# Output projection: three groups of elementwise instructions named for VectorE in place of GpSimd

## The chip, the cores and the metric

One core of a Trainium2 chip runs the whole program. The metric is device time in microseconds (us) of one launch, as the median of several runs. The core has five engines with a queue each: TensorE (in the profile PE, its weight loads PEld) for matrix products, VectorE (DVE) and GpSimd (POOL) for elementwise work, ScalarE (ACT) for copies, casts and activations, and SyncE (SP), which here only issues DMAs. An engine takes its instructions in the order in which they stand in its queue, and an instruction that waits holds everything behind it.

## The reference

The program computes one layer of a hybrid decoder for a prompt of 2048 tokens and for a group of 8 x 4 sampled tokens. Four groups of heads (a convolution, a pooling mixer, stick-breaking attention, cross-attention into memory) each give 512 columns; every group is multiplied by its gate, and what concerns this document is how the layer ends:

```python
mix = jnp.concatenate([y_c * jax.nn.silu(cg), y_p * jax.nn.silu(pg),
                       y_s * jax.nn.silu(sg), y_m * jax.nn.silu(mg)], axis=-1)
out = rms_norm(mix @ w_out, post_g)
return x + out, conv_new, pool_new, k, v
...
y_prompt = rms_norm(xp, final_g)
y_sample = rms_norm(xs, final_g)
```

So `mix`, 2048 (and 32) rows of 2048 columns, is multiplied by `w_out`, 2048 x 1024. The row is normalised and multiplied by the post factor `post_g`, the residual `x` is added, and a last normalisation with the factor `final_g` gives the output. Everything is float32.

## The kernel before

The program runs projections, the sampled group, the prompt's attention and then the output projection, one after another with overlaps; this document is about the last of these, from about 1905 us to the end.

**Seven products in place of eight.** The product `mix @ w_out` is split into 2 x 2 blocks (rows by pairs of 128-row tiles, the 2048 inner columns in halves, the 1024 output columns in halves) and done by the scheme of Strassen and Winograd: seven block products, numbered 1 to 7, of sums and differences of the blocks. Each runs over 8 pairs `i` of row tiles, plus `i = LAST = 8` for the 32 sampled rows, and over two halves `h` of its inner columns. One such `(prod, i, h)` is called a part. A part is 12 matrix products on TensorE (`out_part`, L2020): four blocks of 128 inner columns, each in three passes, since operands are split into a high and a low part (`mh` and `ml` for rows, `wohi` and `wolo` for weights) to keep float32 accuracy.

**What goes before a part.** `out_load` issues the DMA of its rows (`mr`) from DRAM on SP's queue: `mixd` holds `mix`, and `msd` holds differences that an earlier product has stored. `out_combine` makes the sum or difference that the product needs. `out_high` casts it on ACT (L1744, `mh`), `out_low` subtracts (L1755, `ml`, on DVE). In the main loop `prepare` does the load seven parts ahead of the part on TensorE, the combination five and the cast four; `lows` makes the low parts about three ahead. The combinations:

- product 6: L1735 on DVE subtracts in `ts[0]`, pinned behind what was traced on DVE before; L1736 on POOL takes this from a row kept since product 2, in `ts[2]`, which is stored to `msd` and becomes product 3's operand later. `store` issues that DMA on SP once more than two are pending.
- product 5: L1729 on POOL adds the two row halves that product 4's load has brought along (`ts[0] + ts[1]`), queued behind the last L1736 that was traced.
- product 7: L1732 on POOL, which stays as it is.

**What goes after it.** `out_ready` takes the accumulators from PSUM (L1788 to L1807, on DVE), and, where a half of an output tile is complete, has ACT sum its squares (`square`, L1759) and DVE multiply it by the post factor `gpost` (L1812). For the even tiles the left half was finished earlier, by product 2, and was put into DRAM (`c11d`). `out_first` loads it back into `oh` (two buffers), and `out_factor` multiplies it by the post factor: L1840, on POOL. `out_tile` then forms a tile: root of the sum of squares (L1856 to L1858 on DVE and ACT for tiles below 10, L1853 and L1854 on POOL for tiles 10 to 15, into `oss`), scaling and residual (L1864 on DVE), squares again (L1866, ACT), root, final factor (L1871, DVE), and the store.

**Order.** The program is traced part by part, and a planner then arranges each engine's queue by the order of tracing and by when it expects operands to be ready. `tc.keep_in_program_order(ins)` pins an instruction behind the one traced before it on the same engine; `tc.issue_after(ins)` queues what it encloses behind the given one. Anything else may be moved by the planner. The parts run in this order: products 1 and 7 over all `i`; 2 and 6 in turn; then, from `last_` on, 4, 5 and 3 in turn:

```python
order += [(4, 0), (4, 1), (5, 0), (5, 1), (4, 2), (5, 2), (3, 0), (3, 1), (3, 2), (5, 8), (3, 8)]
order += [(p, i) for i in range(3, 8) for p in (4, 5, 3)]
```

So in the last stage each pair of row tiles costs TensorE six parts: two of product 4, two of 5, two of 3.

Of the kernel before, what the change touches and what calls it, by code (L numbers as in the profile page):

```python
# [13 lines left out]
ALU = mybir.AluOpType  # L14
# [78 lines left out]
def kernel(  # L93
# [9 lines left out]
    pe, act, dve, pool, sp = nc.tensor, nc.scalar, nc.vector, nc.gpsimd, nc.sync  # L103
# [1540 lines left out]
    def store(key=None):  # L1644
        while len(stores) > 2 or key in [k for k, *_ in stores]:
            sp.dma_start(*stores.pop(0)[1:])
# [76 lines left out]
    def out_combine(x):  # L1723
        prod, i, h = x
        store()
        ts = raws[x]
        if prod == 5 and i < LAST:
            with tc.issue_after(keep["sixth"]):
                pool.tensor_tensor(out=ts[1], in0=ts[0], in1=ts[1], op=ALU.add)  # L1729
            ts = ts[1:]  # L1730
        elif prod == 7:
            pool.tensor_tensor(out=ts[0], in0=ts[0], in1=ts[1], op=ALU.subtract)  # L1732
            stores.append(((0, i, h), msd[0, i, h], ts[0]))
        elif prod == 6:
            tc.keep_in_program_order(dve.tensor_tensor(out=ts[0], in0=ts[0], in1=ts[1], op=ALU.subtract))  # L1735
            keep["sixth"] = pool.tensor_tensor(out=ts[2], in0=ts[2], in1=ts[0], op=ALU.subtract).ins  # L1736
            stores.append(((1, i, h), msd[1, i, h], ts[2]))
        raws[x] = ts[0]

# [21 lines left out]
    def out_ready(prod, i, o):  # L1761
# [35 lines left out]
        else:  # L1797
# [28 lines left out]
            if prod == 5 and i != 2 or (prod, i) == (3, 1):  # L1826
                out_factor(2 if prod == 3 else i)
# [9 lines left out]
        keep[2 * i, 0] = c  # L1837

    def out_factor(i):
        pool.tensor_tensor(out=keep[2 * i, 0], in0=keep[2 * i, 0], in1=gpost[:, :512], op=ALU.mult)  # L1840

    def out_tile(t, a, b):

# [130 lines left out]
    raws, mix, accs, keep, stores = {}, {}, {}, {}, []  # L1974
# [3 lines left out]
    def side_work():  # L1978
        nonlocal opm, conv
        with tc.tile_pool(name="sm", bufs=1, side="left", reuse_waits="tile") as sm2:  # L1980
            yield from sample_end(sm2, side_ps, S)
        with tc.tile_pool(name="wsp", bufs=1, side="left", reuse_waits="tile") as wsp:
            yield from weight_sums(wsp)
        opm = ox.enter_context(tc.tile_pool(name="opm", bufs=1, side="left", reuse_waits="tile"))
        yield from out_weights(1, opm, pool)
        while (3, 0) not in flags:
            yield
        for x in lead_:
            out_load(x)
            out_combine(x)  # L1990
            out_high(x)
            out_low(x, pool)
            yield

        while (3, 1) not in flags:
            yield
        for x in parts[2 * LEAD : 2 * LEAD + 3]:
            out_load(x)
        cp = cx.enter_context(tc.tile_pool(name="cp", bufs=1, side="left", reuse_waits="tile"))
        conv = conv_post(cp, lambda n: conv_ps[0](n), lambda: cx.enter_context(  # L2000
            tc.tile_pool(name="cpw", bufs=1, side="left", reuse_waits="tile")))
        while "centered" not in flags:
            next(conv)
            yield
# [55 lines left out]
    op = oy.enter_context(tc.tile_pool(name="op", bufs=1, side="right", reuse_waits="tile"))  # L2060
# [58 lines left out]
    def prepare(n):  # L2119
        for d, f in ((3, out_load), (1, out_combine), (0, out_high)):  # L2120
            for x in parts[: n + d]:
                if x in ready[d]:
                    continue
                prod, i, h = x
                if d == 3 and not h and prod == 2:
                    while i < LAST and ("conv", i) not in flags:
                        next(conv, None)
                    if i == LAST:
                        for _ in conv:
                            pass  # L2130
                f(x)
                ready[d].add(x)

    ready = {d: set(lead_ if d < 3 else parts[: 2 * LEAD + 3]) for d in (3, 1, 0, -1)}
    for n, x in enumerate(parts):
        if n == last_:
# [3 lines left out]
            gpost = ope.tile([P, D], F32, name="gpost", bufs=1)  # L2140
# [4 lines left out]
        prod, i, h = x  # L2145
# [55 lines left out]
```

## Time and profile before

| | |
|---|---|
| median of 3 runs | 2331.49 us (2330.65 to 2332.27) |
| the profiled execution: its time | 2334.9 us |
| its span | 2333.2 us |
| mean granted TensorE clock | 0.993 of full speed |
| first and last start of L1736 (POOL, x16) | 2053.1 and 2163.1 us |
| first and last start of L1729 (POOL, x16) | 2167.0 and 2275.8 us |
| first and last start of L1840 (POOL, x8) | 2180.3 and 2297.6 us |

Two kinds of views are used. A group line names the line of the kernel, the engine, the operation, output <- inputs and shapes; then `x` the count, `|` busy time in us, the mean of one in ns, `|` the idle time of the engine just before these, and what ended it. A timeline line is a start in us, a duration in us, the engine, the instruction, and in brackets the idle time before it with what ended it. Times are from the span's start. Busy times are those of instructions; an instruction that is held back by the hardware after its start shows as a longer one, and one that waits for another engine's signal shows as idle time in front of it.

### The profile page before, as it was taken

To read this page: it belongs to the slowest core of one execution; us is meant where nothing else is said; L and a number is where in the kernel's file an instruction comes from. 1 tells how busy PE (TensorE), PEld (TensorE's weight loads), DVE (VectorE), ACT (ScalarE), POOL (GpSimd) and SP (SyncE) were. 2 spreads that over 40 slices of the span, in tenths; PEclk is the share of its full clock that TensorE was granted. 3 is DMA by queue.
4 is the path that set the end of the run, shared out by engine and by line. 5 is a ranking of instruction groups with operands and counts; after the bars stand their busy time and mean duration, and the time that the engine had idled before them with its cause. 6 is when DMAs were issued, how large, how long until landed. Compare 5 with 4: busy or idle time off the path is not lost. (4 is left out here: it accounts for less than half of the span.)

```text
span 2333.2 us, 43434 instructions
## 1 busy us (share of the span) xinstructions
PE 2248.1 (96%) x16512; PEld 1810.3 (78%) x16512; DVE 1659.4 (71%) x2247; ACT 1125.2 (48%) x2031; POOL 1293.5 (55%) x1410
## 2 busy tenths in 40 slices
PE   7999999999999999999999999999999999999997
PEld 7998888898888777777777777666766668788775
DVE  5342786969747764478786868787877766686997
ACT  5332343242442322224242334699999976453553
POOL 3554545556474656545546455498988864332333
PEclk9999999999999999999999999999999999999999
DMA  6689987878778999987977884676554207876774
GB/s 205 206 283 310 339 272 258 287 249 287 246 257 310 307 357 334 334 279 271 318 255 236 296 274 145 171 217 175 153 137 130 73 24 250 274 223 204 237 243 145
DMA packets 338187, 558.31 MB, mean 239 GB/s; under 512 B 29162, under 2 KB 213610, under 8 KB 321580
## 3 DMA queue, kind: packets, MB, share of 16 engines
q1 hardware_dynamic: 282604, 286.83, 39.9%
q0 software_dynamic: 55376, 268.72, 32.6%
q8 instruction: 130, 2.13, 0.4%
q14 instruction: 77, 0.63, 0.1%
HBM read 465.35 MB, written 90.72 MB: 238 GB/s over the span
## 5 line engine op out<-in xcount | busy, mean ns | idle before, releaser
L990 DVE STREAM_TRANSPOSE T<-kt 128x1024 f32<-128x1024 f32 x256 | 308.7, 1226 | 188.1 <-PE sSA L1003 177.1
L957 POOL DMA_INDIRECT vt<-in_cache_v_dram,idv x256 | 252.0, 984 | 257.4 <-PE sO L1042 196.4
L642 DVE SCALAR_TENSOR_TENSOR cacc<-U,par,cacc 128x512 f32<-128x512 f32 x480 | 359.9, 750 | 11.0
L1375 POOL TENSOR_TENSOR be<-be,E 128x512 f32<-128x512 f32 (+4 forms) x316 | 300.9, 962 | 27.1 <-DVE E L1366 8.7
L1366 DVE TENSOR_TENSOR_SCAN E<-gam,cr,ZM 128x513 f32<-128x513 f32 x192 | 232.5, 1265 | 25.1 <-ACT gam L1296 22.0
L957 POOL DMA_INDIRECT kt<-in_cache_k_dram,idk x128 | 128.4, 1003 | 194.6 <-DVE T L990 150.1
L2020 PE MATMUL acc<-wohi,mh 128*128 128x512 f32 (+1 forms) x480 | 193.1, 402 | 0.2 <-ACT mh L1744 0.2
L2020 PE MATMUL acc<-wolo,mh 128*128 128x512 f32 (+1 forms) x480 | 189.0, 394 | 0.7 <-DVE wolo L1655 0.7
L2020 PE MATMUL acc<-wohi,ml 128*128 128x512 f32 x448 | 178.2, 398 | 8.9 <-DVE ml L1755 8.8
L1394 PE MATMUL AT<-ident,be 128*128 128x128 f32 x1082 | 150.7, 278 | 23.2 <-ACT at L1396 19.0
L1396 ACT COPY at<-AT 128x512 f32<-128x512 f32 (+1 forms) x288 | 162.3, 653 | 20.0 <-PE AT L1394 17.2
L1394 PEld LDWEIGHTS AT<-ident,be 128*128 128x128 f32 x1082 | 118.7, 141 | 66.2 <-issue 28.6
L1296 ACT ACTIVATE gam<-S 128x1024 f32<-128x1024 f32 (+1 forms) x158 | 163.4, 1034 | 7.3 <-PE S L1293 4.5
L1297 ACT ACTIVATE be<-S 128x1024 f32<-128x1024 f32 (+1 forms) x158 | 162.7, 1030 | 0.0
L1003 PE MATMUL sSA<-T,W 128*32 128x128 f32 x4096 | 139.6, 276 | 2.5 <-DVE T L990 1.4
L1406 PE MATMUL av<-at,V 128*64 128x256 f32 (+1 forms) x1152 | 135.7, 375 | 0.0
L1292 PE MATMUL S<-kh,Q 128*128 128x512 f32 (+1 forms) x316 | 132.1, 422 | 3.2 <-ACT be L1297 3.2
L1003 PEld LDWEIGHTS sSA<-T,W 128*32 128x32 f32 x4096 | 105.1, 109 | 38.4 <-issue 31.2
L1363 DVE TENSOR_TENSOR_SCAN E<-gam,ZM 128x384 f32<-128x384 f32 (+1 forms) x124 | 95.4, 814 | 53.7 <-ACT gam L1296 50.2
L1755 DVE TENSOR_TENSOR ml<-mr,mh 128x512 fp32r<-128x512 f32 x108 | 94.2, 879 | 42.9 <-ACT mh L1744 42.0
L1042 PE MATMUL sO<-vt,saT 128*32 128x512 f32 x1024 | 122.3, 592 | 0.0
L1406 PEld LDWEIGHTS av<-at,V 128*64 128x64 f32 x1152 | 75.8, 137 | 56.4 <-issue 24.2
(590 smaller groups left out, 6174.2 us busy)
## 6 DMA issues: line engine op xcount, KB each, us to landing
mr<-mixd SPq DMA_DIRECT2D x32, 512.0 KB
Q<-qd SPq DMA_DIRECT2D x96, 128.0 KB
mr<-mixd SPq DMA_DIRECT2D x48, 256.0 KB
xtp<-in_x_prompt_dram SPq DMA_DIRECT2D x16, 512.0 KB
kh<-kd SPq DMA_DIRECT2D x64, 128.0 KB
ws<-in_w_out_dram SPq DMA_DIRECT2D x16, 512.0 KB
wsd<-ws SPq DMA_DIRECT2D x16, 512.0 KB
msd<-mr SPq DMA_DIRECT2D x32, 256.0 KB
```

Source lines behind the costliest of these rows:

```text
L642: dve.scalar_tensor_tensor(out=ps, in0=U[:, a + k : a + k + H], scalar=wd[:, k : k + 1], in1=ps, op0=ALU.mult, op1=ALU.add)
L957: pool.indirect_dma_start(out=dst, out_offset=None, in_=rows, in_offset=bass.IndirectOffsetOnAxis(ap=idx, axis=0))
L990: S["turn"] = dve.transpose(T[:, 2 * hh : 2 * hh + 2].rearrange("p s j t -> p (s j t)"), kt[:, 2 * hh : 2 * hh + 2].rearrange("p s j d -> ...
L1003: pe.matmul(sSs[n][32 * g : 32 * g + 32, P * ml : P * (ml + 1)], lhsT=W[:, jj, :], rhs=T[:, :, jj, :], start=i == 0, stop=i == 3, tile_pos ...
L1296: act.activation(out=ga, in_=S[:, :, :w], func=AF.Sigmoid, scale=-1.0)
L1297: act.activation(out=be, in_=S[:, :, :w], func=AF.Sigmoid)
L1366: dve.tensor_tensor_scan(out=E[:, j][:, ::-1], data0=g_[:, j][:, ::-1], data1=ZM[:, 0:1].to_broadcast([P, 513]), initial=carry[hh, q2][:, ...
L1375: newest.append(pool.tensor_tensor(out=be[:, j, :m], in0=be[:, j, :m], in1=E[:, j, 513 - w : 513 - w + m], op=ALU.mult).ins)
L1394: pe.transpose(ap_[:, n : n + P], A[hp, qb, kc, hh, qt][:, P * r : P * (r + 1)], ident)
L1396: act.copy(at[:, :n], ap_[:, :n])
L1406: pe.matmul(av[64 * hh : 64 * hh + 64, c], lhsT=V[:, 4 * kc + r, 64 * hh : 64 * hh + 64], rhs=ats.pop((hp, qb, kc, hh, q2, r)), start=dg a ...
L2020: pe.matmul(o[:rows], lhsT=m[a][:, k, :rows], rhs=W[prod, 4 * h + k][w], start=not cont and h == k == n == 0, stop=h == 1 and k == 3 and n ...
```

## The change

The instruction of L1729 (16 of them), L1736 (16) and L1840 (8), all 128 x 512 float32 with both inputs in SBUF, is named for VectorE. The first two are pinned in the order of the program; the third isn't. With L1736 on DVE, the queueing of L1729 behind it falls away.

```diff
         if prod == 5 and i < LAST:
-            with tc.issue_after(keep["sixth"]):
-                pool.tensor_tensor(out=ts[1], in0=ts[0], in1=ts[1], op=ALU.add)
+            tc.keep_in_program_order(dve.tensor_tensor(out=ts[1], in0=ts[0], in1=ts[1], op=ALU.add))
             ts = ts[1:]
...
         elif prod == 6:
             tc.keep_in_program_order(dve.tensor_tensor(out=ts[0], in0=ts[0], in1=ts[1], op=ALU.subtract))
-            keep["sixth"] = pool.tensor_tensor(out=ts[2], in0=ts[2], in1=ts[0], op=ALU.subtract).ins
+            tc.keep_in_program_order(dve.tensor_tensor(out=ts[2], in0=ts[2], in1=ts[0], op=ALU.subtract))
             stores.append(((1, i, h), msd[1, i, h], ts[2]))
...
     def out_factor(i):
-        pool.tensor_tensor(out=keep[2 * i, 0], in0=keep[2 * i, 0], in1=gpost[:, :512], op=ALU.mult)
+        dve.tensor_tensor(out=keep[2 * i, 0], in0=keep[2 * i, 0], in1=gpost[:, :512], op=ALU.mult)
```

## What I expected before seeing the result

> **What bounds the kernel now.** I read the page first, then the table of stages for the last 283 us, then the waits of TensorE stage by stage, then the groups of instructions and the timelines of VectorE (DVE) and GpSimd (POOL).
>
> ```profile
> span 2333.2 us, 43434 instructions
> PE 2248.1 (96%) x16512; PEld 1810.3 (78%) x16512; DVE 1659.4 (71%) x2247; ACT 1125.2 (48%) x2031; POOL 1293.5 (55%) x1410
> ```
>
> The stages of the output projection, one line each:
>
> ```profile
> 2050.00:2160.00 110.00, 107.39 (x541) 89.52 (x540) 83.82 (x127) 48.50 (x99) 34.28 (x27) 0.98 0.71 219
> 2160.00:2218.00 58.00, 53.76 (x230) 42.14 (x229) 52.48 (x87) 31.41 (x72) 19.56 (x9) 1.00 0.73 235
> 2218.00:2250.00 32.00, 31.21 (x136) 23.41 (x134) 30.90 (x51) 16.63 (x45) 13.31 (x9) 1.00 0.77 259
> 2250.00:2284.00 34.00, 32.43 (x137) 25.52 (x138) 31.63 (x52) 16.57 (x45) 8.59 (x7) 1.00 0.64 217
> 2284.00:2320.00 36.00, 33.07 (x138) 25.07 (x136) 29.18 (x41) 15.54 (x40) 9.84 (x19) 1.00 0.43 153
> ```
>
> The columns are the stage and its length, then the busy time of PE, PEld, DVE, ACT and POOL, the granted clock, and DMA. TensorE is busy 96% of the span, so a change on other engines can only win what TensorE waits for. From 2160 to 2320 us it was idle 160 less 150.5, that is 9.5 us. DVE in the same four stages was busy 52.5 + 30.9 + 31.6 + 29.2 = 144.2 us of 160, thus 90%, while its share of the whole span is only 71%. These four stages are one: what DVE does is what TensorE waits for, as the waits of TensorE say, for the first, third and fourth of them:
>
> ```profile
> PE acc L2020 <- DVE ml L1755: 3.5, 3, 2.7
> PE acc L2020 <- DVE wolo L1655: 0.7, 1, 0.7
> ```
>
> ```profile
> PE acc L2020 <- DVE ml L1755: 2.4, 3, 1.5
> ```
>
> ```profile
> PE acc L2020 <- DVE ml L1755: 2.6, 4, 1.3
> ```
>
> The columns are the sum in us, the times and the longest. They add up to 9.2 us, nearly all of the 9.5; the second stage has no such row. In every case the low part of a product's rows (`ml`) or of a weight (`wolo`) came late from DVE. So 9.2 us, about 0.4% of the time, is on offer, and not more.
>
> **What POOL costs DVE today.** The timelines around one moved instruction, POOL's first, then DVE's:
>
> ```profile
> 2155.28 1.62 POOL L1736 TENSOR_TENSOR mr<-mr,mr 128x512 f32<-128x512 f32 x1 [2.69 <-DVE mr L1735]
> ```
>
> ```profile
> 2154.46 0.68 DVE L1735 TENSOR_TENSOR mr<-mr 128x512 f32<-128x512 f32 x1
> 2155.06 0.68 DVE L1655 TENSOR_TENSOR wolo<-wor,wohi 128x512 fp32r<-128x512 f32 x1
> 2155.66 1.78 DVE L1735 TENSOR_TENSOR mr<-mr 128x512 f32<-128x512 f32 x1
> 2157.38 0.68 DVE L1755 TENSOR_TENSOR ml<-mr,mh 128x512 fp32r<-128x512 f32 x1
> ```
>
> Undisturbed, DVE starts one 128x512 instruction every 0.60 us (2154.46, 2155.06, 2155.66), and each shows 0.68. The one that starts while POOL has its own two-input instruction shows 1.78: it is held 1.10 us. The same stretching shows in the groups of DVE for 2160 to 2320 us:
>
> ```profile
> L1755 DVE TENSOR_TENSOR ml<-mr,mh 128x512 fp32r<-128x512 f32 x50 | 42.5, 856 | 1.2 <-ACT mh L1744 0.8
> L1871 DVE SCALAR_TENSOR_TENSOR oxt<-oxt,oss,gfin 128x1024 f32<-128x1024 f32 x14 | 19.9, 1423 | 4.2 <-POOL oss L1854 4.2
> L1864 DVE SCALAR_TENSOR_TENSOR oxt<-acc,oss,oxt 128x512 f32<-128x512 f32 x21 | 15.0, 743 | 0.8 <-POOL oss L1854 0.7
> L1655 DVE TENSOR_TENSOR wolo<-wor,wohi 128x512 fp32r<-128x512 f32 x18 | 13.7, 776 | 2.1 <-ACT wohi L1650 2.1
> L1864 DVE SCALAR_TENSOR_TENSOR oxt<-oh,oss,oxt 128x512 f32<-128x512 f32 x7 | 8.3, 1193 | 0.7 <-POOL oss L1854 0.7
> L1856 DVE TENSOR_TENSOR oss<-ssk 128x1 f32<-128x1 f32 x10 | 2.3, 230 | 0.0
> L1856 DVE TENSOR_TENSOR oss<-oss 128x1 f32<-128x1 f32 x10 | 2.0, 196 | 2.2 <-ACT junk L1866 2.2
> L1780 DVE TENSOR_TENSOR both<-both,gpost 32x512 f32<-32x512 f32 x1 | 1.8, 1777 | 0.0
> L1871 DVE SCALAR_TENSOR_TENSOR oxt<-oxt,oss,gfin 32x1024 f32<-32x1024 f32 x1 | 1.3, 1262 | 0.0
> L1856 DVE TENSOR_TENSOR oss<-oss 32x1 f32<-32x1 f32 x1 | 0.1, 141 | 0.0
> ```
>
> Means above the undisturbed duration, times the count: `ml` 50 x (0.856 - 0.68) = 8.8; L1871 14 x (1.423 - 1.262) = 2.3; `wolo` 18 x (0.776 - 0.68) = 1.7; L1864 on `oh` 7 x (1.193 - 0.743) = 3.2; L1780 1.777 - 0.68 = 1.1; the two L1856 groups 0.9 + 0.55 = 1.4. That is **18.5 us** of DVE time lost. The two L1864 groups are the same operation: the one that reads an accumulator in PSUM keeps 743 ns, the one that reads SBUF twice averages 1193. In these 160 us POOL has three large groups, and all of them are what the change moves:
>
> ```profile
> L1729 POOL TENSOR_TENSOR mr<-mr 128x512 f32<-128x512 f32 x16 | 27.1, 1705 | 57.0 <-DVE mh L1755 33.3 <-DMA mr<-mixd 23.5
> L1840 POOL TENSOR_TENSOR oh<-oh,gpost 128x512 f32<-128x512 f32 x8 | 12.7, 1595 | 20.7 <-DMA oh<-c11d 11.1 <-DVE acc L1779 6.2 <-DVE ml L1755 3.4
> L1736 POOL TENSOR_TENSOR mr<-mr,mr 128x512 f32<-128x512 f32 x1 | 4.0, 3958 | 3.9 <-ACT junk L1759 3.9
> ```
>
> So 25 POOL instructions cost DVE 18.5 us, 0.74 each, though they aren't DVE's.
>
> **The change part by part.**
>
> *The subtraction for product 3 (L1736), 16 times, 15 of them in 2050 to 2160.* Groups of that stage, DVE and then POOL:
>
> ```profile
> L1755 DVE TENSOR_TENSOR ml<-mr,mh 128x512 fp32r<-128x512 f32 x27 | 25.2, 937 | 6.6 <-ACT mh L1744 6.2
> L1655 DVE TENSOR_TENSOR wolo<-wor,wohi 128x512 fp32r<-128x512 f32 x13 | 14.4, 1129 | 0.0
> L1735 DVE TENSOR_TENSOR mr<-mr 128x512 f32<-128x512 f32 x14 | 11.2, 808 | 0.0
> ```
>
> ```profile
> L1736 POOL TENSOR_TENSOR mr<-mr,mr 128x512 f32<-128x512 f32 x15 | 22.6, 1510 | 51.1 <-DVE mr L1735 47.6 <-issue 2.7 <-DMA c11d<-c 0.8
> ```
>
> Held time here: 27 x 0.257 + 13 x 0.449 + 14 x 0.128 = 14.6 us. POOL has other work in this stage as well; L1736 is 22.6 of its 34.28 busy us, so I give it two thirds, 9.6 us. Added: the new instruction reads what L1735 has just written, and a pair of that kind shows here:
>
> ```profile
> 2160.89 0.67 DVE L1769 TENSOR_TENSOR both<-both,acc 32x512 f32<-32x512 f32 x1
> 2161.59 0.68 DVE L1773 TENSOR_TENSOR both<-both,both 32x512 f32<-32x512 f32 x1
> ```
>
> 0.70 from start to start, so 15 x 0.70 = 10.5 us. The net is +0.9 us on a DVE that is idle 26 of 110 us there, in which TensorE lost only 2.6 us. I take nothing for it. If that cover failed, the cost would be the 0.9; if the held time alone counted, a gain up to the 2.6. Its store to DRAM leaves after a 0.7 us step in place of 1.5, which only helps the queue of SyncE (SP).
>
> *Sums (L1729, 16) and post factors (L1840, 8), with one last L1736: 25 in 2160 to 2320.* They read rows that came by DMA, not a neighbour's result, so the pitch is 0.60: 25 x 0.60 = 15.0 us added, 18.5 removed, **net -3.5 us**. But it is not spread evenly. POOL runs ahead of the products: in the last stage only one moved instruction was left on it, and it held an `ml` on DVE by 1.1 us:
>
> ```profile
> 2297.61 2.21 POOL L1840 TENSOR_TENSOR oh<-oh,gpost 128x512 f32<-128x512 f32 x1 [0.24 <-DMA oh<-c11d]
> ```
>
> ```profile
> 2298.60 1.76 DVE L1755 TENSOR_TENSOR ml<-mr,mh 128x512 fp32r<-128x512 f32 x1
> ```
>
> On DVE a sum is pinned behind the instruction traced before it, and both are traced five parts ahead of the product; as far as the order of the program holds, the sums of row blocks 6 and 7, four in all, and one to three factors come after 2284. That stage gets 5 to 7 instructions, 3.0 to 4.2 us, and is relieved of 1.1: +1.9 to +3.1, I take +2.5. The three stages before it get -3.5 - 2.5 = **-6.0 us**. TensorE waits for DVE there 3.5 + 0.7 + 2.4 = 6.6 us, so I count the 6.0 in full. In the last stage DVE has gaps that can hide some of the 2.5: L1871 alone waits 4.2 us for `oss`, a chain through ACT and POOL that a sum doesn't lengthen if it falls into the gap. I take half, +1.2. The last factor may fall into the 13 us after the last product, where it costs 0 to 0.6; I take 0, as its DMA has long landed.
>
> *Queues and waits.* No DMA is added and none is moved to another queue. The waits for the rows move from POOL to DVE: behind a sum on DVE stand the `ml` of the next parts, and TensorE waits for those. Bounds: nothing, where DVE comes to the sum after its DMA; up to the 23.5 + 11.1 us that POOL idled until a DMA, where DVE came as early as POOL did. I take nothing, since DVE is behind and not ahead, and keep a part of it as a rival. ACT makes the high part from the sum; a sum now lasts 0.7 in place of 1.7 us.
>
> *Sum:* -6.0 + 1.2 = -4.8 us. The profiled execution took 2334.9 us around its span of 2333.2; the median shown is 2331.49, and a difference of this kind carries over as it is: **2326.7 us**.
>
> **The rivals.**
>
> *All waits of TensorE go* (20%). If DVE's lag vanishes, the 9.2 us go, to **2322.3 us**. For it: 18.5 us is a low count, as rows of other shapes were left out; and the last stage inherits the lead won before. Against it: DVE has 15 us of new work in a stretch where it was idle only 15.8. [...]
>
> *The relief falls where nobody waits* (27%). A good part of the stretching lies in 2218 to 2250, which has no TensorE wait of its own, and the order of DVE's queue, planned anew, may put a sum in front of an urgent `ml`. If half of the 6.0 is won and the whole 2.5 is paid: -0.5; if the gaps help, -2.5. I set **2330.0 us**: within the 0.2%.
>
> *DVE stands at the head of its queue for a DMA* (13%, the other side). The factor isn't pinned, so the planner may let it float to where it expects its rows. The load on SP's queue, the factor on POOL and the tile on DVE that uses the result:
>
> ```profile
> 2278.08 0.32 SPq L1836 DMA_DIRECT2D oh<-c11d x1
> ```
>
> ```profile
> 2280.75 1.31 POOL L1840 TENSOR_TENSOR oh<-oh,gpost 128x512 f32<-128x512 f32 x1 [3.25 <-DMA oh<-c11d]
> ```
>
> ```profile
> 2294.03 0.75 DVE L1864 SCALAR_TENSOR_TENSOR oxt<-oh,oss,oxt 128x512 f32<-128x512 f32 x1 [0.34 <-POOL oss L1854]
> ```
>
> The rows land 2.7 us after issue, and POOL stood waiting for them 3.25 us; the tile that needs the result came 13 us later. If DVE takes the factors as early as POOL did, it inherits their 11.1 us of waiting, and with the relief of 3.5 the time is 2331.5 + 7.6 = **2339.1 us**. The point that decides: DVE must reach the instruction more than about 3 us before its rows land in several of the eight cases. Against it: the program traces the factor after the tile in front, over 5 us behind the load.
>
> That the instructions stay on POOL can't be: the engine is named in each edit.
>
> **How the numbers follow.** About 0.2%, 4.7 us, is what a measurement of this kernel can tell from no change; so faster begins at 2326.8 and slower at 2336.2. My forecast of 2326.7 has 40%; its own spread (2 to 7 us won) lies on both sides of that bound, and I count 25 of the 40 as faster. With the first rival's 20 that is 0.45 faster; the other 15 and the second rival's 27 are 0.42 within; the third's 13 slower. The range runs from 2321.0, just under all waits gone, to 2334.5: the second rival with 4.5 us more, as when one or two waits for rows strike. Outside it are the bulk of the third rival and a few per cent below.
>
> **What would show it.** The number of POOL instructions falls by 40, DVE's rises by 40. The groups L1755 and L1864 on `oh` in the last 160 us go to about 0.68 and 0.75 us, whatever the time does; if they stay stretched, the theory of held instructions is wrong. DVE's busy time in 2160 to 2320 falls by about 3.5 us. TensorE's waits for `ml` shrink before 2284 and not after it. Wrong would be: idle time of DVE in front of the sums or factors that ends with a DMA (third rival), or `ml` waits as before though the stretching is gone (second rival).

## The result and the profile after

| | before | after |
|---|---|---|
| median of the comparison, 6 runs each | 2331.32 us (2329.92 to 2336.15) | 2350.06 us (2347.12 to 2351.24) |
| the profiled execution | 2334.9 us | 2351.24 us |
| its span | 2333.2 us | 2349.5 us |
| ratio after to before | | 1.0066, 95% interval 1.0051 to 1.0081 |

The kernel became **slower**, by 15.4 us of 2331.3 by the ratio (11.9 to 18.9 by its interval; the two medians lie 18.7 us apart), where 4.8 us less was forecast. Of all executions in this document one was in a slow state, 3668.86 us at a granted clock of 0.557 (the kernel without the pin, below), and the ratios leave it out. The lines of the kernel after stand one lower than before from L1728 on: the sum is L1728, the factor L1839, the cast L1743, `ml` L1754, the post factor after a product L1811, the final factor L1870, the matrix products L2019.

The head of the page of after, and its table of stages (the columns as in the prediction):

```profile
span 2349.5 us, 43376 instructions
PE 2251.6 (96%) x16512; PEld 1815.8 (77%) x16512; DVE 1658.5 (71%) x2287; ACT 1127.5 (48%) x2031; POOL 1229.9 (52%) x1370
```

```profile
2160.00:2218.00 58.00, 57.52 (x251) 46.36 (x250) 54.60 (x103) 34.62 (x81) 0.00 (x0) 1.00 0.76 248
2218.00:2250.00 32.00, 23.78 (x93) 17.29 (x92) 25.06 (x50) 13.68 (x36) 0.00 (x0) 0.84 0.71 249
2250.00:2284.00 34.00, 29.51 (x121) 23.10 (x119) 26.58 (x51) 14.85 (x41) 0.00 (x0) 0.95 0.50 170
2284.00:2320.00 36.00, 31.84 (x130) 25.28 (x131) 25.89 (x39) 14.63 (x34) 5.99 (x14) 0.95 0.42 154
```

The change did what it says: 40 instructions fewer on GpSimd, 40 more on VectorE, and VectorE's total is 0.9 us lower in spite of them. Until 2218 us the kernel after is *ahead*: it was busy on TensorE for 57.52 of 58 us, against 53.76 before. Then it loses: from 2218 to 2250 it does 93 matrix products where the kernel before did 136. The granted clock falls too (0.84, 0.95, 0.95, against 1.00 in all four stages before). And VectorE, 90% busy in these stages before, is busy 26.58 of 34 us from 2250 to 2284: it has become idler. What TensorE waits for after 2160 us:

```profile
PE acc L2019 <- ACT mh L1743: 19.0, 5, 8.2
PE acc L2019 <- DVE ml L1754: 0.8, 2, 0.5
```

The waits for `ml`, 9.2 us with `wolo` before, are down to 0.8. In their place stand five waits for **`mh`**, ACT's cast, which no row of before after 2160 us shows. ACT runs 2031 instructions as it did, so something comes late to it.

**Where the five waits come from.** VectorE's timeline around the second of them. An eviction is the step that takes a product's accumulator from PSUM; the first line is that of (3,3), product 3 of row block 3, which completes tile 6, and the second that of (4,4):

```profile
2252.84 0.70 DVE L1806 TENSOR_TENSOR acc<-acc,U 128x512 f32<-128x512 f32 x1
...
2258.31 0.70 DVE L1806 TENSOR_TENSOR acc<-acc,U 128x512 f32<-128x512 f32 x1 [0.32 <-PE acc L2019]
...
2260.50 0.68 DVE L1839 TENSOR_TENSOR oh<-oh,gpost 128x512 f32<-128x512 f32 x1
2261.09 1.28 DVE L1870 SCALAR_TENSOR_TENSOR oxt<-oxt,oss,gfin 128x1024 f32<-128x1024 f32 x1
2262.29 0.68 DVE L1728 TENSOR_TENSOR mr<-mr 128x512 f32<-128x512 f32 x1
2263.71 2.50 DVE L1754 TENSOR_TENSOR ml<-mr,mh 128x512 fp32r<-128x512 f32 x4 [0.74 <-ACT mh L1743]
...
2268.51 0.69 DVE L1798 TENSOR_TENSOR U<-acc,U 128x512 f32<-128x512 f32 x1 [1.69 <-PE acc L2019]
```

The same moment on ACT, and on TensorE:

```profile
2263.06 2.18 ACT L1743 CAST mh<-mr 128x512 fp32r<-128x512 f32 x4 [3.09 <-DVE mr L1728]
```

```profile
2260.60 0.39 PE L2019 MATMUL acc<-wohi,ml 128*128 128x512 f32 x1
2263.73 0.50 PE L2019 MATMUL acc<-wohi,mh 128*128 128x512 f32 x1 [2.75 <-ACT mh L1743]
```

Read from the bottom up. TensorE has finished part (5,4,0) and wants (5,4,1). Its cast starts at 2263.06 and is the first of four that ACT had queued one behind the other (those of the two parts of product 3 and of (4,5,0) follow it): ACT stood idle 3.09 us for the sum. The sum of (5,4,1) started at 2262.29 straight behind an L1870 at 2261.09, by the program's order the final factor of tile 6; it is pinned there, since it is traced when the even tile of the row block in front has just been traced. And L1870 is the end of a tile that starts from a product of TensorE. So there is a loop: **when the eviction of (3,3) starts, at 2252.84, TensorE has three parts left that it can do, 36 products of 0.227 us or 8.2 us; the way from there over the tile's end, the sum and the cast takes 2263.73 - 2252.84 = 10.9 us, and 2.7 us are missing.** In block 4 the eviction of (4,4) stands in this way too: it waited 0.32 us for TensorE, which then had one part left, 2.7 us, against 5.4 us to the product. In blocks 5, 6 and 7 the waits are about as long: 2.74, 2.80 and 2.48 us. But what takes the time differs: in blocks 6 and 7 the eviction of (4,i) waits for nothing, and L1870 waits for the tile's root on GpSimd, here in block 6:

```profile
2303.37 1.28 DVE L1870 SCALAR_TENSOR_TENSOR oxt<-oxt,oss,gfin 128x1024 f32<-128x1024 f32 x1 [1.35 <-POOL oss L1853]
```

In block 3, with the longest wait, the tile is that of the sampled rows. In block 4 the second-half sum holds four casts and four `ml` behind it. VectorE itself then waits for TensorE (1.69 us before L1798), which is why it looks idle.

The chain of work that ended last, of after, shows the last of the five in its own words (start, us, what):

```profile
2322.34 0.30 POOL oss L1852
...
2322.71 0.56 POOL oss L1853
...
2323.30 1.28 DVE oxt L1870
2324.58 0.61 DVE mr L1728
...
2325.27 0.63 ACT mh L1743
...
2325.94 10.07 PE acc L2019 x36
```

The root of a finished output tile (GpSimd), its final factor, then the sum, its cast, and the last 36 products: the end of one row block's tile has come to stand in front of the next row block's product. On GpSimd the last of all sums had started at 2275.8 us (the table of before); here it starts at 2324.50, straight behind that L1870 (the chain counts it from the end of the factor).

**The ledger.** Up to 2160 us the two are level. From the first product after that to the last, before ends at 2319.3 and after at 2335.6 us, 16.3 later, as is the span. TensorE's waits grew from 9.1 to 19.8 us, thus by 10.7. The rest is slower products. I counted the products that started 0.30 to 0.62 us after the one before them with no wait in between: 18 before, 2.2 us over the usual 0.227; 40 after, 8.0 us. That is 5.8 more, and 16.5 in all. (Both traces hold 1408 of these products in all, and the 16.5 miss the 16.3 by 0.2.)

### The profile page after: what moved, and what is told of

It reads as the page before. It is cut to its first block, busy times and chain, and to the rows that moved or that the text cites. A ratio compares the mean times of both kernels' runs of the same rounds, so it can differ in the third digit from the quotient of the medians.

```text
span 2349.5 us, 43376 instructions
## 1 busy us (share of the span) xinstructions
PE 2251.6 (96%) x16512; PEld 1815.8 (77%) x16512; DVE 1658.5 (71%) x2287; ACT 1127.5 (48%) x2031; POOL 1229.9 (52%) x1370
## 5 line engine op out<-in xcount | busy, mean ns | idle before, releaser
L2019 PE MATMUL acc<-wohi,mh 128*128 128x512 f32 (+1 forms) x480 | 195.8, 408 | 19.0 <-ACT mh L1743 19.0
L2019 PE MATMUL acc<-wolo,mh 128*128 128x512 f32 (+1 forms) x480 | 191.0, 398 | 0.0
L2019 PE MATMUL acc<-wohi,ml 128*128 128x512 f32 x448 | 179.2, 400 | 2.0 <-DVE ml L1754 2.0
L1396 ACT COPY at<-AT 128x512 f32<-128x512 f32 (+1 forms) x288 | 162.5, 653 | 21.5 <-PE AT L1394 18.7
L2019 PEld LDWEIGHTS acc<-wohi,mh 128*128 128x128 f32 (+1 forms) x480 | 90.6, 189 | 41.5 <-ACT mh L1743 21.1
L1743 ACT CAST mh<-mr 128x512 fp32r<-128x512 f32 (+1 forms) x120 | 70.0, 599 | 107.1 <-PE acc L2019 35.8
```

Source lines behind the costliest of these rows:

```text
L1396: act.copy(at[:, :n], ap_[:, :n])
L2019: pe.matmul(o[:rows], lhsT=m[a][:, k, :rows], rhs=W[prod, 4 * h + k][w], start=not cont and h == k == n == 0, stop=h == 1 and k == 3 and n ...
```

## The experiments

Theory **place**: the second-half sum on VectorE is late because it stands behind the end of a tile that itself waits for TensorE. Rivals: it is the added work on VectorE (**load**); it is one of the other two parts of the change; it is the pin as such.

### One part of the change alone

The kernel before with just the sums on VectorE, pinned; with just the subtraction; with just the factor.

```diff
 # sums only
-            with tc.issue_after(keep["sixth"]):
-                pool.tensor_tensor(out=ts[1], in0=ts[0], in1=ts[1], op=ALU.add)
+            tc.keep_in_program_order(dve.tensor_tensor(out=ts[1], in0=ts[0], in1=ts[1], op=ALU.add))
 # subtraction only (the sums stay on GpSimd, no longer queued behind it)
-            keep["sixth"] = pool.tensor_tensor(out=ts[2], in0=ts[2], in1=ts[0], op=ALU.subtract).ins
+            tc.keep_in_program_order(dve.tensor_tensor(out=ts[2], in0=ts[2], in1=ts[0], op=ALU.subtract))
 # factor only
-        pool.tensor_tensor(out=keep[2 * i, 0], in0=keep[2 * i, 0], in1=gpost[:, :512], op=ALU.mult)
+        dve.tensor_tensor(out=keep[2 * i, 0], in0=keep[2 * i, 0], in1=gpost[:, :512], op=ALU.mult)
```

> The kernel before with the sums for product 5 alone moved to VectorE, pinned as in the change; the subtractions for product 3 and the post factors stay on GpSimd. Theory 'place': the five waits for the high part are all there and the time is that of the changed kernel or a little more, 2346 to 2353 us. Rival 'order' (the planner's new order as a whole, or one of the other two moves): at least a third of the loss is missing, under 2343 us.

> The kernel before with the subtractions for product 3 alone on VectorE, pinned as in the change; the sums for product 5 stay on GpSimd without the queueing behind those. Theory 'place': within 3 us of the kernel before, 2328 to 2334 us, as VectorE has idle time in that stage. Rival 'order': 2336 us or more.

> The kernel before with the eight post factors alone on VectorE. Theory 'place': no wait of TensorE for the high part over 1 us; the held time of the eight is saved, 2326 to 2332 us. Rival 'order' or a wait for the rows from DRAM at the head of VectorE's queue: 2336 us or more, with idle time of VectorE in front of the factor that ends with a DMA.

| | median | ratio to before (95%) |
|---|---|---|
| sums only | 2363.39 us | 1.0130 (1.0106 to 1.0155) |
| subtraction only | 2332.47 us | 0.9999 (0.9983 to 1.0015) |
| factor only | 2333.54 us | 1.0008 (0.9993 to 1.0023) |

The kernel before in these comparisons: 2332.37 us. TensorE's longest row of waits from 2160 us on with the sums alone:

```profile
PE acc L2019 <- ACT mh L1743: 24.2, 6, 7.5
```

The sums alone make the loss, and a larger one than the whole change: 30 us by the ratio; the median is ten above the top of what I expected. Neither of the others moves the time by more than the measurement can tell. The factor's time is 1.5 us above what I expected of it. With the sums alone there is a sixth wait, of 7.5 us, at row block 2: there the sum starts at 2207.82 straight behind an L1870 at 2206.61, the end of tile 3. TensorE's waits add up to 5.2 us more than in the change, and 65 slow products (counted as in the ledger) cost 13.2 us in place of 8.0: 10.4 of the 13.4 us between the two spans. Three of the last four waits are longer too, 3.05 to 3.61 us. What GpSimd has to do with that shows in VectorE's timeline before the third of the six, and GpSimd's:

```profile
2268.88 2.06 DVE L1870 SCALAR_TENSOR_TENSOR oxt<-oxt,oss,gfin 128x1024 f32<-128x1024 f32 x1
2270.87 0.68 DVE L1728 TENSOR_TENSOR mr<-mr 128x512 f32<-128x512 f32 x1
```

```profile
2268.59 1.28 POOL L1839 TENSOR_TENSOR oh<-oh,gpost 128x512 f32<-128x512 f32 x1 [20.88 <-DMA oh<-c11d]
```

The final factor lasts 2.06 us, where its mean in the kernel after is 1.28, beside a factor that runs on GpSimd, and the sum is behind it. These 0.78 us on VectorE now lie on the path that ends in the sum.

### The sums kept on VectorE, but out of that place

The kernel after, with both sums of a row block traced with its first half, still pinned. There they come before the end of the even tile.

```diff
         if prod == 5 and i < LAST:
-            tc.keep_in_program_order(dve.tensor_tensor(out=ts[1], in0=ts[0], in1=ts[1], op=ALU.add))
+            for t_ in (ts, raws[5, i, 1]) if not h else ():
+                tc.keep_in_program_order(dve.tensor_tensor(out=t_[1], in0=t_[0], in1=t_[1], op=ALU.add))
```

> The changed kernel, but the two sums of a row block for product 5 are both traced with the first half's combination, so the second stands one part earlier on VectorE, in front of the tile that it stood behind. All instructions stay on the engines of the change. Theory 'place' (the second half's sum stands behind the last multiplication of the even tile, and TensorE waits for its cast five times): the five waits of TensorE for the high part (19.0 us in the changed kernel) fall to under 2 us in all, and the time comes to 2323 to 2330 us, below the kernel before, as the held VectorE instructions are gone as well. Rival 'load' (VectorE can't carry 24 more instructions in this stage, wherever they stand): TensorE loses as much as before the move, 2343 to 2350 us.

It took 2326.52 us (2320.57 to 2331.68, 10 runs), ratio 0.9970 (0.9957 to 0.9984). All of TensorE's waits from 2160 us on:

```profile
PE acc L2020 <- DVE ml L1755: 1.1, 1, 1.1
```

The same engines, the same 40 instructions, the same pins: 22 us less than the change as it was made, by the two ratios, and less than before. Only the place of eight sums differs. That rules out *load* as the cause of the loss, and the pin as such.

### The change without the pin on the sums

```diff
-            tc.keep_in_program_order(dve.tensor_tensor(out=ts[1], in0=ts[0], in1=ts[1], op=ALU.add))
+            dve.tensor_tensor(out=ts[1], in0=ts[0], in1=ts[1], op=ALU.add)
```

> The changed kernel with the pin of the sums for product 5 taken away; the order in which the program traces them stays. In VectorE's queue the planner still has each second-half sum of blocks 3 to 7 right behind the last multiplication of an even tile (or of the sampled rows), as in the changed kernel. Theory 'place': the five waits for the high part remain, 16 to 22 us in all, and the time stays 0.5 to 1% above the kernel before. Rival 'pin' (the pin itself holds the sums back): the waits go and the time falls to 2332 us or less.

It took 2324.13 us, ratio 0.9964 (0.9944 to 0.9984). Here my expectation was wrong in what it took for granted: without the pin the planner does *not* keep the second-half sums in the late place. VectorE's timeline of this kernel (taken from its second measurement, below) has the sum of (5,4,1) at 2243.63, 9 us ahead of the end of tile 6, which it directly follows in the change as it was made (the second-half sums of blocks 3, 5, 6 and 7 too are 7 to 13 us ahead of the tile ends that they followed):

```profile
2243.63 0.67 DVE L1728 TENSOR_TENSOR mr<-mr 128x512 f32<-128x512 f32 x1
...
2252.65 1.28 DVE L1870 SCALAR_TENSOR_TENSOR oxt<-oxt,oss,gfin 128x1024 f32<-128x1024 f32 x1
```

So the pin does harm through the place in which it holds the sum, and a pin in another place (the kernel with paired sums) does none. As this is the fastest version, it was measured again, beside one more:

> The changed kernel without the pin on the sums, the same kernel as e1_free, on the chip that runs the kernel beside it and timed in five rounds, since it is the fastest kernel so far (2324.13 us, ratio 0.9964, 0.9944 to 0.9984). Theory 'place': the gain holds, 2321 to 2328 us, ratio 0.995 to 0.9985; the second-half sums stand ahead of the even tile's last multiplication, and no wait of TensorE ends with mh. Rival: the gain of the first time was the chip's spread, and the ratio's interval takes in 1.000.

2322.80 us (2316.67 to 2328.14, 12 runs), ratio 0.9964 (0.9952 to 0.9976): the gain holds. That is 8.4 us by the ratio, 5.6 to 11.2 by the interval. TensorE's waits from 2160 us on:

```profile
PE acc L2019 <- DVE ml L1754: 2.5, 3, 1.2
```

### One row block only

The kernel after with the paired sums for row block 3 alone, where the 8.2 us wait stood; the other blocks as in the change.

```diff
+            for t_ in ((ts, raws[5, i, 1]) if not h else ()) if i == 3 else (ts,):
```

> The changed kernel with the two sums of block 3 alone traced together, one part earlier; blocks 4 to 7 stay as in the change. Theory 'place', with a price for each block: the first wait of 8.2 us goes, and the slow products behind it (some 3 us); the four waits of 2.5 to 2.8 us stay. 8 to 12 us less than the changed kernel, 2336 to 2342 us. Rival 'one cause for all' (a lag of VectorE that builds up at block 3 and is carried on): all five waits go, 2330 us or less; or none goes.

2344.14 us, ratio 1.0058 (1.0041 to 1.0075), missed by 2 us to the slow side. The interval overlaps that of the change (1.0051 to 1.0081), so that the time fell isn't clear of the noise; all waits together fell from 19.8 to 14.1 us. TensorE's timeline, the first of its four waits for `mh`:

```profile
2255.03 0.80 PE L2020 MATMUL acc<-wohi,mh 128*128 128x512 f32 x1 [5.72 <-ACT mh L1744]
```

The wait of block 3 is gone, and that of block 4 is 5.72 in place of 2.75 us; the three after it are 2.74, 2.53 and 2.47. Of 8.2 us about 3 were carried on to the next place of the same kind. The loop gives each block its own wait, and in both kernels the first one met is the longest. My reading, which no run tests, is that the lead that TensorE's operands had until then is used up there.

### More of the same work, in the late place and in the other

The kernel after, with each second-half sum made three instructions long (it adds, takes away and adds again), or each first-half sum.

```diff
+            for op_ in (ALU.add, ALU.subtract, ALU.add) if h == 1 else (ALU.add,):   # the other kernel: h == 0
+                a_, b_ = (ts[1], ts[0]) if op_ == ALU.subtract else (ts[0], ts[1])
+                tc.keep_in_program_order(dve.tensor_tensor(out=ts[1], in0=a_, in1=b_, op=op_))
```

> The changed kernel, where each second-half sum is followed by a subtraction and an addition that give the same sum again: two more VectorE instructions for each of the 8 blocks, 0.70 us each. Theory 'place' (this sum is on the path to TensorE in blocks 3 to 7): each of the five waits grows by about 1.4 us, 6 to 9 us more than the changed kernel, 2354 to 2361 us. Rival 'load': half as much or less, and the same as the next kernel.

> The changed kernel, where each first-half sum is followed by a subtraction and an addition that give the same sum again: the same number of added VectorE instructions as in the kernel before, on the other half. Theory 'place': the first-half sum has a gap of 1.4 to 2.4 us of VectorE behind it in blocks 4 to 7, so nearly nothing, 0 to 2 us more than the changed kernel, 2347 to 2353 us. Rival 'load' (any VectorE time in this stage costs): the same as with the second half.

Longer second halves: 2369.86 us, ratio 1.0155 (1.0131 to 1.0180). Longer first halves, the same number of added instructions: 2352.90 us, 1.0087 (1.0062 to 1.0112), whose interval overlaps that of the change itself. TensorE's waits for blocks 4 to 7 in the kernel with longer second halves, then in that with longer first halves (after itself: 2.75, 2.74, 2.80, 2.48):

```profile
2271.87 0.80 PE L2021 MATMUL acc<-wohi,mh 128*128 128x512 f32 x1 [4.19 <-ACT mh L1745]
...
2295.34 0.80 PE L2021 MATMUL acc<-wohi,mh 128*128 128x512 f32 x1 [4.19 <-ACT mh L1745]
...
2319.56 0.80 PE L2021 MATMUL acc<-wohi,mh 128*128 128x512 f32 x1 [4.75 <-ACT mh L1745]
...
2342.78 0.80 PE L2021 MATMUL acc<-wohi,mh 128*128 128x512 f32 x1 [3.90 <-ACT mh L1745]
```

```profile
2268.78 0.79 PE L2021 MATMUL acc<-wohi,mh 128*128 128x512 f32 x1 [2.74 <-ACT mh L1745]
...
2289.34 0.79 PE L2021 MATMUL acc<-wohi,mh 128*128 128x512 f32 x1 [2.27 <-ACT mh L1745]
...
2308.76 0.50 PE L2021 MATMUL acc<-wohi,mh 128*128 128x512 f32 x1 [1.16 <-ACT mh L1745]
...
2327.61 0.50 PE L2021 MATMUL acc<-wohi,mh 128*128 128x512 f32 x1 [1.37 <-ACT mh L1745]
```

Two more dependent instructions in the late place (three together take 2.12 to 2.14 us, one alone 0.68) lengthen each of these four waits by 1.42 to 1.95 us, about by their own 1.4. The wait of block 3 does not grow: it is 7.40 in place of 8.22 us, behind a sixth wait of 3.42 us at row block 2, which the change did not have. I expected 2354 to 2361 for this kernel, and it went 9 us over: TensorE waits 29.3 us in all in place of 19.8, and 81 slow products in place of 40 cost 16.0 us in place of 8.0, counted as in the ledger.

The same two instructions in the other place lengthen none of the five waits for `mh` (block 3 has 4.80 us). That kernel has a new wait of 6.2 us for `ml` at 2202 us, whose cause stays open; all its waits from 2160 us on add up to 19.3 us, no more than in the change.

### The sums alone, in the good place

The kernel before with just the paired sums on VectorE; subtraction and factors stay on GpSimd.

> The kernel before, with only the sums of rows moved to VectorE, both sums of a row block traced with its first half; the subtraction of row block 6 and the eight factors stay on GpSimd. Theory 'place' (a second-half sum on VectorE stands behind the even tile's last multiplication, and TensorE waits for the casts): the place is gone, so the waits of TensorE for ACT mh come to under 2 us in all, against 24.2 us in the kernel with the sums alone moved. GpSimd keeps eight factors and one subtraction, about 9 x 0.74 = 6.7 us of held time on VectorE, against none after the whole change with paired sums: 2324 to 2333 us, ratio 0.997 to 1.001 against before. [...]

2328.31 us, ratio 0.9990 (0.9977 to 1.0002). Its waits from 2160 us on:

```profile
PE acc L2020 <- DVE ml L1755: 3.4, 3, 2.6
PE acc L2020 <- DVE wolo L1655: 0.7, 1, 0.7
```

No wait for `mh`, against 24.2 us with the sums in the late place: 1.0130 to 0.9990, some 33 us, for the place of eight instructions. With all three parts and the sums in the same place the ratio was 0.9970 (0.9957 to 0.9984); the two intervals overlap, so that the other two parts add a gain is not shown.

## Why the prediction was wrong

**Wrong is the step "Queues and waits".** It said of the wait on VectorE: "I take nothing, since DVE is behind and not ahead". The step looked at one kind of wait only, that of the moved instruction for its own rows, and priced it from GpSimd's waits for DMAs. On that it was right: after has no idle time at all before the sums or the factors (groups of VectorE, 2160 to 2326 us):

```profile
L1754 DVE TENSOR_TENSOR ml<-mr,mh 128x512 fp32r<-128x512 f32 x48 | 31.8, 683 | 6.0 <-ACT mh L1743 6.0
...
L1728 DVE TENSOR_TENSOR mr<-mr 128x512 f32<-128x512 f32 x16 | 10.9, 681 | 0.0
L1839 DVE TENSOR_TENSOR oh<-oh,gpost 128x512 f32<-128x512 f32 x8 | 5.4, 675 | 0.0
L1863 DVE SCALAR_TENSOR_TENSOR oxt<-oh,oss,oxt 128x512 f32<-128x512 f32 x7 | 5.2, 747 | 0.7 <-POOL oss L1853 0.7
```

What it never asked is what the instruction waits for *behind which* the sum is pinned. The text had the pieces: the pin, "the instruction traced before it", and "the `ml` of the next parts" behind it. It did not name that instruction (the final factor of the even tile), nor set its time against the part's due time. In place of nothing the runs show 19.0 us of waits of TensorE for the cast behind that sum, and 5.8 us of slower products after them. And its count of parts was one off: the combinations are traced four parts ahead, counted from the part just finished, not five (the same count in the section on the kernel before). With the right count the second-half sum (5,i,1) comes straight after (3,i-1,1), the part that completes the even tile, and TensorE has three parts, 8.2 us, from there to its due time; in these fit that tile's evictions, squares, two roots and final factor, and then the sum and the cast, only if nothing else gets in between. The planner put the eviction of (4,i) in between, whose operand is ready after two of the three parts, and other steps as well; which of them makes the way too long was not tried, and in blocks 6 and 7 it isn't a wait of this eviction.

**Right were the steps on held time.** `ml` went to 683 ns (856 before), L1863 on `oh` to 747 (1193 before), as foretold. The last 160 us were to net -3.5 us on VectorE. Busy time from 2160 us to the end, in which both do the same work, before and then after:

```profile
2160.00:2333.00 173.00, 150.48 (x638) 116.14 (x636) 150.73 (x235) 83.76 (x212) 55.66 (x49) 0.97 0.62 207
```

```profile
2160.00:2349.00 189.00, 156.18 (x641) 122.27 (x639) 147.17 (x259) 85.91 (x212) 11.99 (x24) 0.92 0.55 189
```

150.73 - 147.17 = 3.6 us, with 24 instructions more on VectorE. The stretching went with GpSimd's instructions, whose busy time here fell from 55.66 to 11.99 us.

**The split at 2284** (-6.0 counted in full, +1.2 after it) can't be read in after, where every stage has moved. Its sense, that VectorE's lag is what TensorE waits for and that relief there is gained time, is borne out by the kernel with free sums: 8.4 us gained of a forecast 4.8, close to the first rival's 9.2. The kernel with paired sums, which keeps the pins, gained 7.0 us (3.7 to 10.0), so whether 4.8 was too low stays open. What made the result of the other sign is the one term set to nothing.

**The stage from 2050 to 2160** was taken as 0: after reaches 2160 us level with before, and the subtraction alone gives 0.9999.

**The rivals.** "All waits go" describes the waits for `ml`, not the time. "The relief falls where nobody waits" is not what happened. The third, on the slower side, had the right engine and a wait that holds the queue, but a DMA as its cause, which the rows above exclude, and a price of 2339.1 us. What came is a fourth: a sum tied to the end of a tile. The sign "TensorE's waits for `ml` shrink before 2284" came true while the time rose; it was no test of the time, since a wait for something else can take its place.

## What to carry to other kernels

When an instruction moves to the queue of another engine, write down what it will stand behind there and what *that* waits for, and set the sum of that chain against the due time of whoever needs the result; a queue with little in it lets an instruction run early, and that lead is lost without a row for it in the profile of before (here the last sum started at 2275.8 us on GpSimd and at 2324.50 on VectorE). An instruction whose operands are early should be traced early or left for the planner to place: a pin behind the end of a pipeline stage ties the next stage to it, in a loop that can cost a wait in every round (here 2.48 to 8.22 us in each of five row blocks). Here the change was worth a gain of 0.30% (paired sums) or a loss of 0.66%, and the difference was the place of eight instructions of 0.68 us.

## What the hardware did that I had not expected

**Most of TensorE's five waits for `mh` cost more than their length.** The products after the 2.75 us wait, TensorE's timeline of after:

```profile
2264.46 0.80 PE L2019 MATMUL acc<-wohi,ml 128*128 128x512 f32 x1
2265.05 0.63 PE L2019 MATMUL acc<-wohi,mh 128*128 128x512 f32 x1
2265.48 0.63 PE L2019 MATMUL acc<-wolo,mh 128*128 128x512 f32 x1
...
2267.19 0.59 PE L2019 MATMUL acc<-wohi,ml 128*128 128x512 f32 x1
2267.61 0.39 PE L2019 MATMUL acc<-wohi,mh 128*128 128x512 f32 x1
```

The pitch goes to 0.43 us, from about 2264.2 to 2267.6, and back to 0.23; the granted clock of just these 3.4 us is 0.50. After the 8.2 us wait it lasted from 2241.7 to 2247.1, also at a granted clock of 0.50; after the waits of 2.74 and 2.48 us from 2285.0 to 2288.1, at 0.50, and from 2325.9 to 2329.1, at 0.51. Not each wait did it: after 2.80 us at 2306 in after, and 2.68 us at 2204 in before, only a product or two came late, and the granted clock of the 3.4 us after them is 1.00:

```profile
2204.56 0.50 PE L2020 MATMUL acc<-wohi,ml 128*128 128x512 f32 x1 [2.68 <-DVE ml L1755]
2204.91 0.39 PE L2020 MATMUL acc<-wohi,mh 128*128 128x512 f32 x1
```

So waits of 2.48 to 2.75 us were followed by such a stretch in three cases of after, and two waits of about that length, 2.80 and 2.68 us, were not. The slower products account for 5.8 of the 16.3 us of the ledger. The granted clock and the pitch change together; why they do so after some waits and not after others, no run shows.

**Waits for the same reason did not add up.** With the longest one removed (row block 3) the next grew by 3 us (from 2.75 to 5.72), and the sums alone lost twice what the whole change lost (ratios 1.0130 and 1.0066), though they are the only one of its three parts that loses by itself.
